# A hybrid decoder layer on one core: last shifted tokens gathered in a tile and stored as rows, and one page of indexer keys per unit

## The chip, the cores and the metric

The kernel runs on one core of a Trainium2 chip. The metric is the time of one execution on the device in microseconds (us); the median of three runs is given. Engines are named as in the profile: PE (TensorE matmul; PEld its weight load), DVE (VectorE), ACT (ScalarE), POOL (GpSimd) and SP (SyncE, which here issues nearly all DMAs).

## The reference, cut to what matters

One inference step of one layer: a prompt of 2048 tokens and, beside it, eight samples of one new token each. The layer projects its input once and splits the columns between two groups of heads, a sparse attention and an RWKV-7 recurrence; their outputs are concatenated, projected and added back.

```python
def rwkv_branch(xs, prev_row, S0, gate, mu_shift, ...):
    prev = concatenate([prev_row, xs[:, :-1]], axis=1)   # each token beside the one before
    xm = xs + mu_shift * (prev - xs)                     # the token shift
    r, k, v, wd, ad = split(xm, [512, 1024, 1536, 1600])
    ...
    S_new, y = wkv_scan(S0, r, decay, k_mod, v, -kk, kk * a_h)
    ...
    return out, S_new, xs[:, -1:]                        # xs[:, -1:] is shift_prompt

# samples: the attention's indexer reads all past keys, through a table of pages
kidx_all = concatenate([cache_kidx[page_table].reshape(8, 4096, 64), ki_s], axis=1)
```

Two things here concern the change. `xs` has 1664 columns, which the kernel holds as 13 chunks of 128 (four each for r, k and v, one for wd and ad), and its last token, `xs[:, -1:]`, is an output of 1664 numbers, `shift_prompt`. And the samples' indexer keys are gathered page by page, 32 gathers of 256 KB, before the samples' scores can be computed.

## The kernel before, in words

The prompt's tokens are cut in eight stretches `u` of 256 tokens. The RWKV heads go in four pairs `p` of heads, so that the first long phase of the program, up to about 1455 us, runs over 32 units (p, u). Each unit goes through five steps. `g_front` projects the three shifted chunks of the pair and its gate (fp16 matmuls with a high and a low part, L196 and L204), writes the result into the tile `raw` with the chunk's columns on partitions and 257 tokens along the free axis, and mixes each token with the one before it (`xm`, L512). `g_elem` computes decay and normalisations. `g_chunk` multiplies within chunks of 16 tokens and sends the small matrices through DRAM: eight stores into `asc` (L643), eight loads into `As` (L647), then on POOL a chain of one copy (L650) and 15 pairs of a multiply (L655) and an add (L656) that solves a triangular system in `Us`, then eight stores into `tsc` (L658) and one load into `TT` (L661). `g_inv` transposes `TT` (L672 on DVE) and finishes the inverse with matmuls on PE (L680 to L708). `g_tail` updates the state (L772), makes the output (L782 to L814) and stores it (`mixd`, L815). Between these steps stand pieces of other projections as fillers; weights are prefetched through `wst` (load L178, conversions on ACT L181 and DVE L182). `out_ki_p`, `Kd`, `qTd`, `gd`, `vd` and `wdad` are intermediate results or outputs that other jobs store. After the units come the sparse attention of the prompt, with the samples' work as its background, and the output projection; this second phase runs from about 1460 us to the end, and no line of it is changed.

The order on each engine is not written out by hand. A scheduler sets it from the code's order, from priorities (`later(n)` moves a piece by n) and from a timeline that it works out; `after(x, [y])` adds that x must stand behind y in the order. At run time every engine works through its own list strictly in order, and SP's list is one queue: a DMA whose condition isn't met holds every DMA behind it.

**The last tokens.** At the last stretch of each pair (u = 7) `g_front` stores the last token of each of the three chunks straight from `raw` (L518): a column of 128 partitions with one number of 4 bytes each, into 512 contiguous bytes of `out_shift_p`. One more such column, of the chunk that all pairs share, is stored by `g_ad` (L469). That makes 13 DMAs. `raw` has one buffer: the next pair's `g_pair` begins by setting its first token to zero on DVE (memset L489), and that must wait until the stores of the pair before have read it.

**The pages.** `s_pages` is a generator that gathers one page of the samples' indexer keys per step: an indirect DMA issued by POOL into the tile `pg` (L1461), then an SP store of the tile into `kxd` in DRAM (L1462). `pg` has one buffer, so that each gather waits for the store before it. `g_phase` takes two steps (`PG = 2`) in each unit, but the scheduler has issued all 32 by 468 us. `kxd` is first read (L1472) at 1482 us.

The samples' own shifted row, `out_shift_s<-sx` (L1702), is another output with another layout, and isn't changed. `So` (L789) is the small tile through which a pair's final state leaves, with one buffer in the pool `be`.

Of the kernel before, what the change touches and what calls it, by code (L numbers as in the profile page):

```python
# [9 lines left out]
F32 = mybir.dt.float32  # L10
# [6 lines left out]
OP = mybir.AluOpType  # L17
# [14 lines left out]
GT = 256  # L32
# [8 lines left out]
class Kern:  # L41
# [166 lines left out]
    def phase_g(self):  # L208
# [7 lines left out]
        with ExitStack() as es:  # L216
# [107 lines left out]
                prefetch()  # L324
            for _ in pages:
                pass
            self.A.activation(self.sg, self.sgr, AF.Tanh, scale=0.5)
            V.tensor_scalar(self.sg, self.sg, 0.5, 0.5, op0=OP.mult, op1=OP.add)
            V.tensor_tensor(self.sg, self.sg, self.sgr, op=OP.mult)
# [30 lines left out]
    def consts_g(self, bs):  # L360
# [33 lines left out]
                    self.A.activation(self.lor[i, 2 + n], t[i], AF.Copy, scale=WS)  # L394

        self.wdad = self.dr.tile([128, 3, T], F16, name="wdad")
        self.raw12 = bs.tile([128, GT + 1], F32, name="raw12")
        V.memset(self.raw12[:, 0:1], 0.0)
        self.lwx = bs.tile([128, NCH, 65], F32, name="lwx")
# [49 lines left out]
    def g_ad(self, u, w):  # L449

        V, A, SY = self.V, self.A, self.SY
        sl = slice(u * GT, (u + 1) * GT)
        raw, out = self.raw12, self.be.tile([128, GT], F32, name="wo", tag="ta", bufs=1)
        (pg, _, _), = self.gemm_u(u, w, [self.sx[:, 12]])
        if u:
            V.tensor_copy(raw[:, 0:1], raw[:, GT:])
        A.activation(raw[:, 1:], pg, AF.Copy, scale=1.0 / WS)
        A.activation(out, pg, AF.Copy, scale=self.omu[:, 12:13])
        V.scalar_tensor_tensor(out, raw[:, 0:GT], self.pb[:, 12:13], out, op0=OP.mult, op1=OP.add)
        A.activation(out[0:64], out[0:64], AF.Tanh)  # L460
        hl = self.be.tile([128, 2, GT], F16, name="whl", tag="ksq", bufs=1)
        A.copy(hl[:, 0], out)
        self.G.tensor_tensor(hl[:, 1], out, hl[:, 0], op=OP.subtract)
        for j in range(2):
            for d in range(2):
                SY.dma_start(self.wdad[64 * d:64 * d + 64, j, sl], hl[64 * j:64 * j + 64, 0])
        SY.dma_start(self.wdad[:, 2, sl], hl[:, 1])
        if u == T // GT - 1:
            SY.dma_start(self.a["o_shift_p"][12 * 128:13 * 128].rearrange("(p o) -> p o", o=1), raw[:, GT:])  # L469

    def g_ga(self, j, i, w):

# [19 lines left out]
    def g_front(self, st, u, w0, w1):  # L492
# [20 lines left out]
                if 2 * b + c0 + n == 4:  # L513
                    self.silu(gate, pg[:, (n - 1) * GT:])
        if u == T // GT - 1:
            for j in range(3):
                c0 = (4 * j + p) * 128
                SY.dma_start(self.a["o_shift_p"][c0:c0 + 128].rearrange("(p o) -> p o", o=1), raw[:, j, GT:])  # L518
        return dict(st=st, u=u, xm=xm, gate=gate, i=p * (T // GT) + u)

    def rsqrt(self, x):
# [86 lines left out]
    def g_chunk(self, cx):  # L608
# [35 lines left out]
                         UA[16 * n:16 * n + 16, n // 4, :, :, 0, q:q + 16].rearrange("p a h t -> p (a h) t"))  # L644
        As = bv.tile([128, 16, 16], F32, name="As", bufs=2)
        for n in range(8):
            SY.dma_start(As[16 * n:16 * n + 16], bass.AP(tensor=asc.tensor, offset=asc.offset + 1024 * n,  # L647
                                                         ap=[[0, 4], [256, 4], [1, 256]]))
        Us = bv.tile([128, 4, 16], F32, name="Us", bufs=2)
        G.tensor_copy(Us, self.uinit)  # L650
# [1 line left out]
        for j in range(15):  # L652
            m, w = j // 4 + 1, 15 - j
            sh = [128, m, w]
            G.tensor_tensor(Ut[:, 0:m, j + 1:], bc(As[:, j:j + 1, j + 1:], sh), bc(Us[:, 0:m, j:j + 1], sh), op=OP.mult)  # L655
            G.tensor_tensor(Us[:, 0:m, j + 1:], Us[:, 0:m, j + 1:], Ut[:, 0:m, j + 1:], op=OP.add)  # L656
        for n in range(8):
            SY.dma_start(bass.AP(tensor=tsc.tensor, offset=tsc.offset + 16 * n * 256 + 16 * (n % 4),  # L658
                                 ap=[[256, 4], [64, 4], [1024, 4], [1, 16]]), Us[16 * n:16 * n + 16])
# [786 lines left out]
    def s_pages(self, p):  # L1446
# [11 lines left out]
        yield  # L1458
        for n in range(32):
            t = p.tile([128, 512], F32, name="pg", bufs=1)  # L1460
            G.indirect_dma_start(out=t, out_offset=None, in_=rows, in_offset=bass.IndirectOffsetOnAxis(ap=it[:, n:n + 1], axis=0))  # L1461
            SY.dma_start(self.kxd[n // 4, 8 * (n % 4):8 * (n % 4) + 8].rearrange("j (q d) k -> (j q) (d k)", q=16), t)  # L1462
            yield

    def s_scores(self, p):
        nc, V, A, G, PE, SY = self.nc, self.V, self.A, self.G, self.PE, self.SY
# [366 lines left out]
PB = 6  # L1833
P_LD = -3000
P_SC = 0
FILL = lambda k: 4 + (52 * (k + 1) + 28) // 29
F0, F1 = 1, 4
YB = 2
PG = 2
XTB, SQB = 3, 3  # L1840
X0 = 2
SQP = (0, 2)
# [217 lines left out]
```

## Time and profile before

| | |
|---|---|
| time, median of 3 runs | 2457.18 us (2455.85 to 2461.61) |
| profiled execution | 2460.94 us |
| its span in the trace | 2459.1 us, mean granted PE clock 0.925 |
| PE busy | 2108.7 us, 86% |
| DVE, ACT, POOL busy | 1611.1, 1060.8, 1097.0 us |
| the units' phase, about | 0 to 1455 us |
| stores `out_shift_p<-raw` | 13, of 0.5 KB each |
| page gathers and page stores | 32 and 32, of 256 KB each |

The page of the profile lists busy times, which are sums over the whole span; the waits, the chain of work that ended last and the table by windows tell at which place an engine stood and what released it. In a row of the windows stand the window, its length, then for PE, PEld, DVE, ACT and POOL the busy time with the number of instructions, then the TensorE clock granted (1.00 is full speed), the busy share of the 16 DMA engines, and GB/s. In a row of the timeline stand the start, the time, the engine, the line and operation, and in brackets how long the engine had idled and what ended it.

### The profile page before, as it was taken

To read this page: it belongs to the slowest core of one execution; us is meant where nothing else is said; L and a number is where in the kernel's file an instruction comes from. 1 tells how busy PE (TensorE), PEld (TensorE's weight loads), DVE (VectorE), ACT (ScalarE), POOL (GpSimd) and SP (SyncE) were. 2 spreads that over 40 slices of the span, in tenths; PEclk is the share of its full clock that TensorE was granted. 3 is DMA by queue.
4 is the path that set the end of the run, shared out by engine and by line. 5 is a ranking of instruction groups with operands and counts; after the bars stand their busy time and mean duration, and the time that the engine had idled before them with its cause. 6 is when DMAs were issued, how large, how long until landed. Compare 5 with 4: busy or idle time off the path is not lost.

```text
span 2459.1 us, 55537 instructions
## 1 busy us (share of the span) xinstructions
PE 2108.7 (86%) x20799; PEld 1497.6 (61%) x20799; DVE 1611.1 (66%) x4998; ACT 1060.8 (43%) x2243; POOL 1097.0 (45%) x2841
## 2 busy tenths in 40 slices
PE   6788998699998999979998756998887789888997
PEld 1656777587776788868876432455555445455553
DVE  4883576586775766767876776867787744556531
ACT  1652223232332333322322345888767543665530
POOL 2311345334343243232343326357767765577722
PEclk9898999899999999989999676999889999998999
DMA  6435332311112211132111412312000033220133
GB/s 223 153 113 133 96 106 92 85 51 34 33 48 42 54 51 36 49 62 58 42 37 27 130 29 70 101 58 64 10 27 10 18 84 97 65 59 27 49 104 100
DMA packets 232537, 167.59 MB, mean 68 GB/s; under 512 B 108327, under 2 KB 193280, under 8 KB 232129
## 3 DMA queue, kind: packets, MB, share of 16 engines
q1 hardware_dynamic: 226817, 149.27, 21.8%
q0 software_dynamic: 3328, 10.49, 1.6%
q8 instruction: 165, 2.70, 0.5%
q10 hardware_dynamic: 2112, 4.19, 0.5%
q14 instruction: 115, 0.94, 0.1%
HBM read 113.87 MB, written 50.00 MB: 67 GB/s over the span
## 4 chain that ended last, share of the span: by engine, by line
PE 33%; POOL 22%; DVE 11%; DMA 11%; issue 9%; SPq 7%; ACT 5%; POOLq 0%; DVEq 0%; ACTq 0%
PE ps_g L196 8%; PE ps_s L1341 5%; SPq L647 3%; POOL Us L656 3%; POOL Ut L655 3%; PE ps_l L1031 3%; PE ps_v L1281 2%; PE ps_g L204 2%; PE ps_t L1273 2%; SPq L658 2%; PE ps_g L159 2%; ACT bias L1092 2%; DMA As<-asc 1%; DVE sc L1049 1%; PE ps_e L622 1%
## 5 line engine op out<-in xcount | busy, mean ns | idle before, releaser
L196 PE MATMUL ps_g<-h,w 128*128 128x256 f16 (+1 forms) x4032 | 512.0, 281 | 34.0 <-ACT sgr L356 8.1
L196 PEld LDWEIGHTS <-w 128*128 128x128 f16 x4032 | 394.7, 101 | 105.0 <-issue 31.2
L204 PE MATMUL ps_g<-w,h 128*128 128x256 f16 (+1 forms) x2304 | 251.8, 263 | 3.0 <-ACT nat L848 2.4
L655 POOL TENSOR_TENSOR Ut<-As,Us 128x12 f32<-128x12 f32 (+10 forms) x480 | 130.8, 273 | 260.1 <-DMA As<-asc 217.7
L1252 DVE CUSTOM_DVE_ANT_0 P<-ps_l,bias 128x1024 f32<-128x1024 f32 (+7 forms) x192 | 172.5, 908 | 106.2 <-PE ps_l L1031 61.4
L204 PEld LDWEIGHTS <-h 128*128 128x128 f16 (+1 forms) x2448 | 210.1, 99 | 35.9 <-issue 8.1
L1273 PE MATMUL ps_t<-cf,P 128*128 128x128 f32 x1088 | 185.3, 298 | 32.4 <-ACT P L1260 21.4
L1276 ACT COPY pT<-ps_t 128x512 f32<-128x512 f32 (+1 forms) x288 | 154.0, 560 | 128.7 <-PE ps_t L1273 125.3
L1049 DVE SCALAR_TENSOR_TENSOR sc<-r,wi,sc 128x1024 f32<-128x1024 f32 (+7 forms) x154 | 167.7, 1089 | 37.2 <-ACT r L1048 36.4
L1260 ACT ACTIVATE P<-P,mx 128x1024 f32<-128x1024 f32 (+7 forms) x192 | 171.5, 896 | 39.9 <-DVE mx L1258 39.6
L1273 PEld LDWEIGHTS ps_t<-cf,P 128*128 128x128 f32 x1088 | 130.0, 149 | 89.7 <-ACT P L1260 28.3
L1281 PE MATMUL ps_v<-pT,Vn 128*64 128x128 f32 x2176 | 162.7, 292 | 21.8 <-ACT pT L1276 21.2
L1341 PE MATMUL ps_s<-wo,mt 128*128 128x512 f16 x768 | 172.4, 379 | 7.8 <-DVE t L1345 6.3
L1048 ACT ACTIVATE r<-ps_l 128x1024 f32<-128x1024 f32 (+7 forms) x176 | 142.4, 816 | 76.4 <-PE ps_l L1031 48.5
L1031 PE MATMUL ps_l<-K,qiT 128*128 128x512 f16 (+3 forms) x608 | 154.9, 379 | 23.7 <-ACT r L1048 12.3
L1031 PE MATMUL ps_l<-K,qT 128*128 128x512 f16 (+3 forms) x640 | 155.4, 365 | 19.2 <-ACT r L1048 12.9
L1281 PEld LDWEIGHTS ps_v<-pT,Vn 128*64 128x64 f32 x2176 | 123.2, 143 | 70.3 <-ACT pT L1276 36.8
L1092 ACT ACTIVATE bias<-sc,sm 128x640 uint8<-128x640 f32 (+13 forms) x84 | 109.9, 1308 | 129.5 <-POOL sm L1123 113.3
L656 POOL TENSOR_TENSOR Us<-Us,Ut 128x12 f32<-128x12 f32 (+10 forms) x480 | 133.9, 279 | 34.7
L1341 PEld LDWEIGHTS <-mt 128*128 128x128 f16 x768 | 74.7, 98 | 96.0 <-issue 9.0
L1031 PEld LDWEIGHTS <-qT 128*128 128x128 f16 x640 | 64.7, 104 | 79.5 <-issue 40.8
L1031 PEld LDWEIGHTS <-qiT 128*128 128x128 f16 x608 | 61.6, 106 | 83.2 <-issue 48.9
(561 smaller groups left out, 4234.2 us busy)
## 6 DMA issues: line engine op xcount, KB each, us to landing
wst<-in_wt SPq DMA_DIRECT2D x60, 256.0 KB
xt<-in_xT SPq DMA_DIRECT2D x16, 512.0 KB
wa<-in_w_ada SPq DMA_DIRECT2D x8, 1024.0 KB
kxd<-pg SPq DMA_DIRECT2D x32, 256.0 KB
qTd<-qo SPq DMA_DIRECT2D x32, 256.0 KB
kx<-kxd SPq DMA_DIRECT2D x64, 128.0 KB
mt<-mixd SPq DMA_DIRECT2D x16, 512.0 KB
x<-in_x SPq DMA_DIRECT2D x32, 256.0 KB
```

Of the source, the lines that this page charges most:

```text
L196: self.PE.matmul(out, w[:, a, k], h[:, b, k], start=(n == 0), stop=(n == 3 * KD - 1))
L204: self.PE.matmul(out, h[:, b, k], w[:, a, k], start=(n == 0), stop=(n == 3 * KD - 1))
L655: G.tensor_tensor(Ut[:, 0:m, j + 1:], bc(As[:, j:j + 1, j + 1:], sh), bc(Us[:, 0:m, j:j + 1], sh), op=OP.mult)
L656: G.tensor_tensor(Us[:, 0:m, j + 1:], Us[:, 0:m, j + 1:], Ut[:, 0:m, j + 1:], op=OP.add)
L1031: self.PE.matmul(ps[:, j:j + m], qs, self.K[:, kk, c0 + j:c0 + j + m], start=st, stop=not st)
L1049: self.dve = V.scalar_tensor_tensor(sc[:, c:c + n], r[:, :n], wi[:, h:h + 1], self.tz[:, c:c + n] if h == 0 else sc[:, c:c + n], op0=OP.mu ...
L1092: self.after(A.activation(ja[:, :L], sc[:, :L], AF.Sign, bias=t, accum_out=col(5)), [self.act])
L1252: self.dve = V.tensor_tensor_reduce(P[n][:, :w], pl[:, :w], bias[:, c:c + w], scale=1.0, scalar=-3.0e38, op0=OP.add, op1=OP.max, accum_out ...
L1260: self.act = A.activation(P[n][:, :w], P[n][:, :w], AF.Exp, scale=0.125, bias=mx[:, h, 2:3], accum_out=sums[:, n, h:h + 1])
L1273: PE.transpose(pt[:, q:q + 128], Ps[g][k // 8][:, k % 8 * 128:(k % 8 + 1) * 128], self.ident)
L1281: mm = PE.matmul(pv[64 * g:64 * g + 64, hh * 128:(hh + 1) * 128], self.Vn[:, k, 64 * g:64 * g + 64], pT[:, q + g * 128:q + g * 128 + 128], ...
L1341: PE.matmul(pg, mt[:, b, k], self.wo[:, a, k, js], start=(n == 0), stop=(n == 3 * KD - 1))
```

## The change

The 13 column stores go. A tile `shp` of 128 partitions and 13 columns takes the last tokens instead: DVE copies one column in `g_ad` and three columns at once in `g_front`, at the same places at which the stores were issued. When the loop over the units has been written, one PE transpose turns `shp` into 13 rows of 128, DVE copies these out of PSUM into `sho`, and one SP store writes 13 rows of 512 bytes. `sho` uses the buffer of `So` (tag "So", one buffer), and the three steps have a priority 40 places earlier (`P_SH`).

The pages go one per unit (`PG = 1`) instead of two. Each gather must stand behind the last add of the newest unit's `Us` chain (`h_us`), and each store is issued a unit later, behind the last `As` load (`h_as`) of that next unit's `g_chunk`.

```diff
 g_phase, behind the loop over units:
+            with self.later(P_SH):
+                pt = self.bank("m", 2)
+                PE.transpose(pt[0:13, 0:128], self.shp, self.ident)
+                t = self.be.tile([13, 128], F32, name="sho", tag="So", bufs=1)
+                V.tensor_copy(t, pt[0:13, 0:128])
+                SY.dma_start(self.a["o_shift_p"].rearrange("(c p) -> c p", p=128), t)
 setup:
+        self.shp = bs.tile([128, 13], F32, name="shp")
 g_ad:
         if u == T // GT - 1:
-            SY.dma_start(self.a["o_shift_p"][12 * 128:13 * 128].rearrange("(p o) -> p o", o=1), raw[:, GT:])
+            V.tensor_copy(self.shp[:, 12:13], raw[:, GT:])
 g_front:
         if u == T // GT - 1:
-            for j in range(3):
-                c0 = (4 * j + p) * 128
-                SY.dma_start(self.a["o_shift_p"][c0:c0 + 128].rearrange("(p o) -> p o", o=1), raw[:, j, GT:])
+            V.tensor_copy(self.shp[:, p:p + 9:4], raw[:, :, GT])
 g_chunk:
-            SY.dma_start(As[16 * n:16 * n + 16], ...)
+            self.h_as = SY.dma_start(As[16 * n:16 * n + 16], ...)
...
-            G.tensor_tensor(Us[:, 0:m, j + 1:], Us[:, 0:m, j + 1:], Ut[:, 0:m, j + 1:], op=OP.add)
+            self.h_us = G.tensor_tensor(Us[:, 0:m, j + 1:], Us[:, 0:m, j + 1:], Ut[:, 0:m, j + 1:], op=OP.add)
 s_pages:
         for n in range(32):
             t = p.tile([128, 512], F32, name="pg", bufs=1)
-            G.indirect_dma_start(out=t, ..., in_=rows, in_offset=...)
-            SY.dma_start(self.kxd[...], t)
+            ld = G.indirect_dma_start(out=t, ..., in_=rows, in_offset=...)
+            self.after(ld, [self.h_us])
             yield
+
+            st = SY.dma_start(self.kxd[...], t)
+            self.after(st, [self.h_as])
 constants:
+P_SH = -40
-PG = 2
+PG = 1
```

In the rows below the line number stands first; the lines of the changed kernel have moved down by 5 to 9, so that L643, L647, L658 and L661 of before are L648, L652, L663 and L666 there, and L1461 and L1462 are L1466 and L1470.

The first place is SP's queue at the end of the second pair (p = 1, u = 7). Before:

```order
L518 DMA out_shift_p<-raw 128x1
L815 DMA mixd<-ym 256x1x256
L643 DMA asc_77<-UA 16x4x16 x8
L647 DMA As<-asc_77 16x1x256 x8
L518 DMA out_shift_p<-raw 128x1 x2
L178 DMA wst<-in_wt 128x512 x6
L658 DMA tsc_79<-Us 16x4x16 x8
```

The same place in the changed kernel:

```order
L648 DMA asc_77<-UA 16x4x16 x8
L652 DMA As<-asc_77 16x1x256 x8
L1470 DMA kxd<-pg 128x512
L178 DMA wst<-in_wt 128x512 x2
L820 DMA mixd<-ym 256x1x256
L178 DMA wst<-in_wt 128x512 x2
L663 DMA tsc_79<-Us 16x4x16 x8
```

The three column stores are gone, and a page's store stands behind the eight `As` loads, where none stood in this unit before.

The second place is POOL's list in one of the first units. Before, a gather stands inside the `Us` chain (and two more in the rest of the same chain):

```order
L655 TENSOR_TENSOR Ut<-As,Us 128x15
L656 TENSOR_TENSOR Us<-Us,Ut 128x15
L655 TENSOR_TENSOR Ut<-As,Us 128x14
L656 TENSOR_TENSOR Us<-Us,Ut 128x14
L655 TENSOR_TENSOR Ut<-As,Us 128x13
L1461 DMA pg<-in_kidxT,pgi 128x512
L656 TENSOR_TENSOR Us<-Us,Ut 128x13
```

In the changed kernel the end of a chain, and what follows it:

```order
L661 TENSOR_TENSOR Us<-Us,Ut 128x4x2
L660 TENSOR_TENSOR Ut<-As,Us 128x4
L661 TENSOR_TENSOR Us<-Us,Ut 128x4
L1466 DMA pg<-in_kidxT,pgi 128x512
L904 TENSOR_TENSOR ru<-nat,cg 128x128
L905 TENSOR_TENSOR rv<-nat,cg 128x8x8
```

The chain is unbroken, and one gather stands behind its last add, ahead of POOL's other work of the unit (`ru` and `rv` belong to a rotary job) and of the next unit's chain.

The third place is DVE's list in the last unit (`gx` is the group normalisation of the unit's output `Y`). Before:

```order
L795 TENSOR_REDUCE gx<-ps_m 128x4
L789 COPY So<-ps_m 64x128
L796 TENSOR_SCALAR gx<-gx 128x4
L799 TENSOR_TENSOR UA<-ps_m,gx 128x256
L803 TENSOR_REDUCE gx<-Y 128x4
L804 TENSOR_SCALAR gx<-gx 128x4
```

In the changed kernel:

```order
L800 TENSOR_REDUCE gx<-ps_m 128x4
L794 COPY So<-ps_m 64x128
L801 TENSOR_SCALAR gx<-gx 128x4
L804 TENSOR_TENSOR UA<-ps_m,gx 128x256
L808 TENSOR_REDUCE gx<-Y 128x4
L331 COPY sho<-ps_m 13x128
L809 TENSOR_SCALAR gx<-gx 128x4
```

The copy into `sho` stands between the second reduction and the rest of the normalisation, four rows behind the copy into `So` whose buffer it takes over.

More of the change, by code (lines that the diff above doesn't have):

```diff
@@ L646, in g_chunk @@
         for n in range(8):
-            SY.dma_start(As[16 * n:16 * n + 16], bass.AP(tensor=asc.tensor, offset=asc.offset + 1024 * n,
+            self.h_as = SY.dma_start(As[16 * n:16 * n + 16], bass.AP(tensor=asc.tensor, offset=asc.offset + 1024 * n,
                                                          ap=[[0, 4], [256, 4], [1, 256]]))
@@ L1460, in s_pages @@
             t = p.tile([128, 512], F32, name="pg", bufs=1)
-            G.indirect_dma_start(out=t, out_offset=None, in_=rows, in_offset=bass.IndirectOffsetOnAxis(ap=it[:, n:n + 1], axis=0))
-            SY.dma_start(self.kxd[n // 4, 8 * (n % 4):8 * (n % 4) + 8].rearrange("j (q d) k -> (j q) (d k)", q=16), t)
+            ld = G.indirect_dma_start(out=t, out_offset=None, in_=rows, in_offset=bass.IndirectOffsetOnAxis(ap=it[:, n:n + 1], axis=0))
+            self.after(ld, [self.h_us])
             yield
+            st = SY.dma_start(self.kxd[n // 4, 8 * (n % 4):8 * (n % 4) + 8].rearrange("j (q d) k -> (j q) (d k)", q=16), t)
+            self.after(st, [self.h_as])
     def s_scores(self, p):
```

## The prediction

> **What bounds the kernel now.** I read the busy times by windows over the two phases first, then PE's timeline for its idle gaps, then the waits and the chain of work at each gap.
>
> ```profile
> 220.00:420.00 200.00, 190.35 (x2097) 156.65 (x2098) 125.02 (x416) 55.81 (x140) 75.43 (x198) 0.95 0.36 106
> 800.00:1075.00 275.00, 270.00 (x3361) 223.52 (x3356) 197.63 (x664) 94.83 (x235) 97.95 (x296) 1.00 0.18 47
> 1460.00:2459.00 999.00, 831.84 (x6087) 487.70 (x6087) 608.83 (x1680) 573.70 (x1074) 607.52 (x1478) 0.92 0.20 58
> ```
>
> PE is the bound: in an ordinary stretch of the units it works 190.35 of 200 us (with pages) and 270.00 of 275 us (without); in the attention's phase it works 831.84 of 999. What it loses in the units' phase it loses in a few gaps. These five windows lie one in each gap:
>
> ```profile
> 210.00:215.00 5.00, 0.00 (x0) 0.00 (x0) 0.00 (x0) 0.00 (x0) 0.00 (x0) 0.59 0.99 49
> 450.00:455.00 5.00, 0.00 (x0) 0.00 (x0) 0.43 (x1) 0.00 (x0) 1.80 (x3) 0.50 0.93 46
> 785.00:790.00 5.00, 0.00 (x0) 0.00 (x0) 0.00 (x0) 0.00 (x0) 3.71 (x17) 0.77 1.28 34
> 1080.00:1085.00 5.00, 0.00 (x0) 0.00 (x0) 0.00 (x0) 0.00 (x0) 3.67 (x18) 0.63 0.96 20
> 1345.00:1350.00 5.00, 0.00 (x0) 0.00 (x0) 0.00 (x0) 0.00 (x0) 0.00 (x0) 0.75 0.46 51
> ```
>
> PE, ACT and DVE stand nearly still, while the DMA engines count as busy (0.93 to 1.28 in four of five) and move 20 to 51 GB/s, which is what they move at a share of 0.18 in the ordinary stretch (47 GB/s). Something small is holding all sixteen. PE's rows that end these gaps:
>
> ```profile
> 216.75 0.61 PE L196 MATMUL ps_g<-h,w 128*128 128x256 f16 x2 [8.14 <-ACT sgr L356]
> ...
> 458.85 0.64 PE L708 MATMUL ps_t<-TT,g 32*32 32x32 f32 x16 [13.47 <-ACT g L704]
> 463.43 2.07 PE L622 MATMUL ps_e<-AV,BK 64*128 64x128 f32 x8 [3.94 <-DVE UA L627]
> ...
> 794.55 0.64 PE L708 MATMUL ps_t<-TT,g 32*32 32x32 f32 x16 [11.56 <-ACT g L704]
> ...
> 1089.27 0.43 PE L680 MATMUL ps_t<-tr,UA 16*32 16x32 f32 x14 [10.86 <-DVE ko L889]
> ...
> 1354.44 0.53 PE L680 MATMUL ps_t<-tr,UA 16*32 16x32 f32 x18 [11.53 <-DVE tr L672]
> ```
>
> Together 8.14 + 17.41 + 11.56 + 10.86 + 11.53 = 59.5 us. What stands behind each gap, from the waits, SP's and ACT's timelines and the chain:
>
> ```profile
> 206.00 0.46 SPq L469 DMA_DIRECT2D out_shift_p<-raw  x1
> 206.54 0.39 SPq L178 DMA_DIRECT2D wst<-in_wt  x1
> 216.07 0.63 ACT L181 ACTIVATE w<-wst 128x512 f16<-128x512 f32 x1 [10.10 <-DMA wst<-in_wt]
> ...
> 433.55 10.00 issue
> ...
> DVE gx L795 <- DMA out_shift_p<-raw: 14.4, 1, 14.4
> ...
> DVE gx L530 <- DMA out_shift_p<-raw: 12.0, 1, 12.0
> 1078.45 8.66 DMA out_shift_p<-raw
> ...
> 1343.66 10.04 DMA out_shift_s<-sx
> ...
> 1344.36 0.33 SPq L661 DMA_DIRECT2D TT<-tsc  x1
> DVE tr L672 <- DMA TT<-tsc: 72.4, 25, 12.4
> ...
> 1059.96 1.45 DMA tsc<-Us
> 1061.61 2.06 DMA TT<-tsc
> 205.10 2.09 DMA kxd<-pg
> ```
>
> Every gap follows a column store. Away from these stores a `TT` load lands in 2.06 us and a 256 KB page store in 2.09 us; two column stores of 512 bytes each take 8.66 us. The harm takes three forms. At 785 and 1080 us DVE waits outright (14.4 and 12.0 us; these rows name `gx`, but beside them stands the memset L489 of `raw`'s next pair, which must not run before the stores have read it). At 210 and 1345 us nobody needs the store, but a DMA issued just behind it is late: `wst` of 206.54 keeps ACT until 216.07, `TT` of 1344.36 keeps DVE 12.4 us. At 450 us both meet the pages: SP is held 10.00 us by a page store whose gather is late, the `tsc` stores stand behind it, and then two more column stores surround the `TT` load.
>
> The Trainium skill has a rule that speaks against this reading: its page "DMA: Bandwidth & Descriptors", section "Anatomy of one DMA — SWDGE (gpsimd) path", gives a DMA some 2 us plus bytes by 436 GB/s, for another issuing path, so 512 bytes would cost about 2 us and block nothing. The trace disagrees with 8.66 us for the pair. By the rule it would be the second rival below.
>
> **The change part by part.** First, 13 stores less. The idle time that returns is each gap less what is late next. At 210 us: `wst` behind no column store should land like other 256 KB transfers, between 2.09 us (page store) and 3.4 us (page gather, row below); 206.0 + 3.4 = 209.4, ACT could begin 6.7 us sooner, and I take 6.1. At 450 us: the hold of 10.00 us and the late `TT` go; left are the `tsc` and `TT` landings of 1.45 + 2.06, some 3 of the 17.41 us with the rest of PE's work, so 14.4. At 785 us no DMA is needed for DVE to go on; 1 us left, 10.6. At 1080 us likewise, where nearly all of the 10.86 is one wait, 10.5. At 1345 us the same `tsc` and `TT` landings and 0.6 us for the transpose are left, 4.1 us, so 7.4. Sum 49.0.
>
> Second, the clock. After each gap PE works at a lower granted clock:
>
> ```profile
> 216.00:225.00 9.00, 7.09 (x33) 4.37 (x33) 3.24 (x6) 3.26 (x7) 0.97 (x1) 0.53 0.71 208
> 458.00:470.00 12.00, 7.21 (x56) 6.06 (x56) 8.10 (x22) 4.22 (x10) 2.40 (x2) 0.50 0.48 136
> 794.00:800.00 6.00, 5.45 (x48) 3.98 (x50) 4.46 (x17) 3.14 (x8) 0.00 (x0) 0.67 0.42 119
> 1088.00:1100.00 12.00, 9.05 (x106) 6.62 (x107) 9.02 (x36) 4.23 (x12) 1.51 (x5) 0.57 0.42 109
> 1354.00:1380.00 26.00, 22.45 (x237) 18.32 (x238) 20.64 (x81) 5.63 (x17) 1.39 (x5) 0.50 0.83 268
> ```
>
> PE's busy time times the missing clock is 3.3, 3.6, 1.8, 3.9 and 11.2 us. More than DVE leaves free in the window (its length less DVE's busy time: 5.8, 3.9, 1.5, 3.0, 5.4) can't return, so at most 3.3 + 3.6 + 1.5 + 3.0 + 5.4 = 16.8. Since short gaps stay, I take two thirds, 11. The Trainium skill ("TensorE: Matmul & The Clock Gate", section "What's actually happening") puts the restart at some 3.4 us at half rate, which would make 1.7 us each and 8.5 us in all; the rows at 1.00 elsewhere and 0.50 here agree in kind and show longer restarts, 26 us of it in the last.
>
> Third, the pages. Before, they load the first ten units; now one goes with each unit.
>
> ```profile
> POOL pg L1461 <- DMA kxd<-pg: 80.6, 20, 12.8
> L1461 POOL DMA_INDIRECT pg<-in_kidxT,pgi x32: 943/990/1514, 189.0 to 463.4; - x32
> DMA to landing us min/median/max: 3.2/3.4/4.3
> L1462 SPq DMA_DIRECT2D kxd<-pg x32: 319/332/446, 192.8 to 467.7; - x32
> ...
> L500 DVE COPY raw<-raw x28: 105/169/630, 124.8 to 1317.0; 128x3 f32<-128x3 f32 x28
> ...
> POOL Ut L655 <- DMA As<-asc: 217.7, 25, 23.2
> ```
>
> Gone from the first units are the 80.6 us for which POOL stood inside or between its chains and the SP holds of the page stores. PE hardly felt it: it idles 9.65 of 200 us with pages and 5.00 of 275 without, so at the second rate 200 us would have 3.6, so at most 9.65 − 3.6 = 6 us return; I take 2, since the hold at 433.55 is counted already. In the later units, some 24, each page adds 0.99 us to POOL behind its chain and 0.33 us to SP behind `As`. POOL's cover is its own wait for `As`, 217.7 us in 25 units or 8.7 us each; without that cover a later chain would start 0.99 us later, 24 us in all as the far end. The page stands a unit in its buffer, so the store finds it landed and holds nobody on SP: behind it stand `wd`, `gd`, `mixd` and `wst`, and then `tsc`, which waits for POOL's whole chain. I take 0. The traffic of a page beside the `tsc` stores and the `TT` load has no row of its own: the bounds are 0 and its landing of 3.4 us (a rival below). Near 0 is the nearer row, because the units from 220 us carried three pages each and PE still worked 190.35 of 200 us.
>
> Fourth, what is added. Five DVE copies of at most three columns cost 0.17 us each by the row of `raw`'s own three-column copy, so under 1 us. At the end stand a transpose, a copy and a store:
>
> ```profile
> 1454.41 0.65 SPq L790 DMA_DIRECT2D out_S_p<-So  x1
> 1455.53 0.42 DVE L803 TENSOR_REDUCE gx<-Y 128x4 f32<-128x256 f32 x1 [0.54 <-ACT Y L802]
> ```
>
> `sho` takes `So`'s buffer, so DVE waits there for the landing of the store issued at 1454.41. Issue 0.65 and a landing of 1.45 to 2.09 give 1456.5 to 1457.2; DVE arrives at 1455.95, waits 0.6 to 1.2 us and copies 0.3. Behind it stand the rest of `gx` and the output of the last unit, on the path: 1.5 us. The two last gathers stand back to back, the second waiting for the first one's store, about 2.1 us on POOL beside the attention's start: 0.5 us. Together 2 us.
>
> The attention phase is reordered by the scheduler though no work is added. PE idles 167 of its 999 us there, and a reorder can give some of that back or add to it; I allow a tenth, 17 us, either way for the range and take 0, since nothing in the rows says which.
>
> Sum: −49 − 11 − 2 + 2 = −60. Against the profiled execution of 2460.94 us (span 2459.1) that is 2401; the median of the runs lies 3.8 us below that execution, and I say 2400. A measurement of this kernel can tell about 0.3%, 7.4 us, from no change.
>
> **The rivals.**
>
> *Only the outright waits go.* What is late next at 210, 450 and 1345 us is no column store but the queue itself: six `wst` loads, the `K` loads, or the `tsc` and `TT` chain. For it: at 1345 us the DMA share is 0.46, half of the other gaps', and the chain names `out_shift_s` with 10.04 us, a store that stays. Against it: `out_shift_s` has 104 numbers, 416 bytes, per partition, not 4, and three column stores of the pair stand just ahead of it in SP's queue. Then only 10.6 + 10.5 return with two thirds of 4.5 us of clock (1.5 + 3.0) and 2 of pages: −26, giving 2434.
>
> *The column stores are not the cause.* If 13 stores of 512 bytes block nothing, the gaps stay wherever something else holds the DMA engines, and what goes is the page's hold of 10.00 us: 2450. Against it: two DVE waits named by the trace for these stores, and gaps at 785 and 1080 us where no page runs.
>
> *Slower: a page beside every inverse.* The gather is issued just as the eight `tsc` stores and the `TT` load of the same unit go out. DVE waits for `TT` in 25 units already, 2.9 us each. If the page's 3.4 us go onto this wait and PE stands for it, 24 further units cost 82 us: 2461 − 60 + 82 = 2483. It decides from 60 / 24 = 2.5 us a unit. Against it: PE's share with three pages a unit.
>
> *More than forecast.* All of the 59.5 us, all 16.8 of clock and 6 of pages return, with 2 us of cost: −80, giving 2381.
>
> **How the numbers follow.** The forecast of about 2400, within 17 us for the attention's reorder: 0.68. Only the outright waits: 0.14. More: 0.06. Column stores not the cause: 0.07, half of it within 0.3%. Page beside every inverse: 0.05, of which a fifth stays near no change. Faster 0.68 + 0.14 + 0.06 + 0.035 = 0.915, same 0.045, slower 0.04. The range reaches down to the full return, 2380 in round numbers, and up over the outright waits alone, 2436; above it lie 0.12, below some 0.04.
>
> **What would show it.** In the trace of the changed kernel no `out_shift_p<-raw` row; the windows at the five pair ends filled, with no PE gap over 5 us there; granted clock 0.9 or more behind them; the memset of `raw` with no wait; first phase ending near 1395 us instead of 1455. The wait for `TT` at or below 72.4 us. It would be wrong if gaps of 8 us or more remain with `wst`, `K` or `TT` as releaser, if the wait for `TT` grows by 60 us, or if the attention phase lengthens by over 17 us.

## The result, and the profile after

The changed kernel takes 2375.62 us (median of 4 runs, 2372.52 to 2376.78), against 2456.51 us before (4 runs): a ratio of 0.9665, 95% interval 0.9648 to 0.9681. It is faster, by 81 us where the prediction said 57, and lies 4 us under the range. The profiled execution took 2375.91 us with a span of 2374.1; the two spans differ by 85.0 us.

The same windows as before, over the places where the columns had been stored, and the one long gap of PE that is left, from the windows and PE's timeline of the changed kernel:

```profile
205.00:215.00 10.00, 7.81 (x67) 6.08 (x65) 3.04 (x6) 3.33 (x7) 0.00 (x0) 1.00 0.57 170
415.00:435.00 20.00, 16.18 (x203) 12.63 (x201) 17.64 (x54) 9.75 (x24) 5.12 (x6) 0.83 0.35 101
725.00:740.00 15.00, 15.00 (x220) 12.96 (x219) 8.58 (x28) 6.99 (x20) 5.31 (x21) 1.00 0.29 85
1005.00:1020.00 15.00, 11.83 (x145) 10.29 (x146) 9.30 (x37) 2.52 (x8) 3.56 (x12) 1.00 0.33 96
1315.00:1325.00 10.00, 0.00 (x0) 0.00 (x0) 0.00 (x0) 0.00 (x0) 7.37 (x33) 0.69 0.33 94
```

```profile
1326.15 0.65 PE L685 MATMUL ps_t<-tr,UA 16*32 16x32 f32 x32 [11.89 <-DVE tr L677]
```

Four of the five places hold work again: PE is busy for 78 to 100% of them, at a granted clock of 0.83 to 1.00, where it had stood still. The fifth is as empty as before. To see where the time went I cut each execution at the four copies of a pair's final state (`So`), which stand at the end of each pair in every order, and sum the windows between them. Before, then after:

```profile
170.00:602.28 432.28, 384.77 (x4313) 318.61 (x4311) 276.07 (x933) 134.92 (x329) 155.91 (x408) 0.94 0.31 84
602.28:892.17 289.89, 265.16 (x3348) 217.28 (x3347) 201.46 (x696) 95.32 (x232) 100.62 (x296) 0.96 0.20 47
892.17:1202.35 310.18, 292.64 (x3672) 244.88 (x3673) 222.35 (x817) 96.03 (x255) 104.34 (x343) 0.97 0.20 49
1202.35:1454.11 251.76, 211.46 (x2755) 158.28 (x2753) 182.72 (x597) 83.92 (x196) 81.95 (x257) 0.87 0.20 54
```

```profile
170.00:565.37 395.37, 378.20 (x4329) 313.83 (x4328) 276.30 (x939) 134.68 (x328) 132.02 (x376) 0.97 0.22 61
565.37:836.13 270.76, 262.66 (x3369) 216.74 (x3367) 205.33 (x700) 97.39 (x237) 112.72 (x312) 0.99 0.23 64
836.13:1134.05 297.92, 287.94 (x3624) 241.46 (x3624) 216.34 (x810) 92.53 (x246) 115.20 (x352) 0.99 0.24 66
1134.05:1384.31 250.26, 212.13 (x2756) 159.78 (x2753) 182.91 (x600) 84.75 (x200) 91.71 (x264) 0.87 0.25 71
```

The second number of a row is the pair's length, the third PE's busy time. The pairs became shorter by 36.9, 19.1, 12.3 and 1.5 us, 69.8 in all. PE's idle time in them (length less busy time) fell from 47.5, 24.7, 17.5 and 40.3 us to 17.2, 8.1, 10.0 and 38.1; the clock rose in the first three and not in the last. The remaining 15 us came off the attention's phase, from PE's first matmul after its first long wait (1479.91 before, 1410.51 after) to the end: 979.2 us before, 963.6 after.

### The profile page after: what moved, and what is told of

Read it like the earlier page. It is cut to its first block, busy times and chain, and to the rows that moved or that the text cites. A ratio compares the mean times of both kernels' runs of the same rounds, so it can differ in the third digit from the quotient of the medians.

```text
span 2374.1 us, 55529 instructions
## 1 busy us (share of the span) xinstructions
PE 2094.2 (88%) x20800; PEld 1486.4 (63%) x20800; DVE 1614.7 (68%) x5004; ACT 1059.1 (45%) x2243; POOL 1110.7 (47%) x2841
## 4 chain that ended last, share of the span: by engine, by line
PE 41%; POOL 20%; DVE 11%; issue 8%; DMA 8%; SPq 7%; ACT 5%; POOLq 0%; DVEq 0%; ACTq 0%
PE ps_g L196 9%; PE ps_s L1346 6%; PE ps_l L1036 4%; PE ps_g L204 3%; POOL Ut L660 3%; POOL Us L661 3%; PE ps_v L1286 3%; SPq L652 3%; PE ps_t L1278 2%; PE ps_g L159 2%; PE ps_e L627 2%; DMA As<-asc 2%; SPq L663 2%; SPq L648 1%; ACT bias L1097 1%
## 5 line engine op out<-in xcount | busy, mean ns | idle before, releaser
L196 PE MATMUL ps_g<-h,w 128*128 128x256 f16 (+1 forms) x4032 | 502.2, 277 | 26.4 <-ACT h L453 7.0
L660 POOL TENSOR_TENSOR Ut<-As,Us 128x12 f32<-128x12 f32 (+10 forms) x480 | 135.2, 282 | 302.1 <-DMA As<-asc 269.7
L1286 PE MATMUL ps_v<-pT,Vn 128*64 128x128 f32 x2176 | 161.8, 290 | 25.6 <-ACT pT L1281 25.2
L1036 PE MATMUL ps_l<-K,qiT 128*128 128x512 f16 (+3 forms) x608 | 157.7, 386 | 22.6 <-DVE mx L1257 12.8
L1036 PE MATMUL ps_l<-K,qT 128*128 128x512 f16 (+3 forms) x640 | 155.4, 367 | 13.9 <-ACT r L1053 9.5
L661 POOL TENSOR_TENSOR Us<-Us,Ut 128x12 f32<-128x12 f32 (+10 forms) x480 | 130.9, 273 | 34.7
```

Of the source, the lines that this page charges most:

```text
L196: self.PE.matmul(out, w[:, a, k], h[:, b, k], start=(n == 0), stop=(n == 3 * KD - 1))
L661: self.h_us = G.tensor_tensor(Us[:, 0:m, j + 1:], Us[:, 0:m, j + 1:], Ut[:, 0:m, j + 1:], op=OP.add)
L1036: self.PE.matmul(ps[:, j:j + m], qs, self.K[:, kk, c0 + j:c0 + j + m], start=st, stop=not st)
L1286: mm = PE.matmul(pv[64 * g:64 * g + 64, hh * 128:(hh + 1) * 128], self.Vn[:, k, 64 * g:64 * g + 64], pT[:, q + g * 128:q + g * 128 + 128], ...
```

## The experiments

All are told by the same two lengths of their profiled execution: the end of the units' phase (the last `So` copy) and the attention's phase as just defined. In these comparisons the kernel before took 2449 to 2453 us instead of 2456.5, so times are compared as ratios to it. Where I say that PE's order is the same, the list of its instructions is the same row for row. Each length is that of one execution. Two executions of before's order, `before` and `before_bg1300` (told below), end the units' phase at 1454.1 and 1443.3 us, and two of the changed kernel's order, the changed kernel and `after_bg1300`, at 1384.3 and 1389.0. So a difference of less than some 10 us between two single executions shows little.

### The two halves of the change

`shift_only` is the changed kernel with the pages put back:

```diff
-            ld = G.indirect_dma_start(...); self.after(ld, [self.h_us])
-            yield
-            st = SY.dma_start(self.kxd[...], t); self.after(st, [self.h_as])
+            G.indirect_dma_start(...); SY.dma_start(self.kxd[...], t)
+            yield
-PG = 1
+PG = 2
```

> The gathered last tokens alone; the pages as before, two per unit. Theory (the column stores hold the DMA engines, and the pages in the first units cost some 12 us beside that): the gaps at the ends of pairs 1 and 2 go (-19 and -12 us, as in the changed kernel), the first pair gives back some 25 of the 37 us, the last pair 2, and the attention's phase, which the scheduler orders anew in every variant, lies within 15 us either way: 2398, between 2383 and 2413. Rival (the pages make the gaps of the first pair, the column stores only DVE's two waits): -33, 2424.

`pages_only` is the kernel before with the pages of the change and the 13 column stores.

> One page per unit alone; the 13 column stores as before. Theory: DVE's waits of 12 to 14 us at the memset of raw stay, the windows at the pair ends stay empty, only the first pair's pages give back some 12 us: 2445, between 2430 and 2460 with the attention's reorder. Rival: -37 at the first pair, nothing more, 2420.

Measured: `shift_only` 2382.46 us, ratio 0.9724 (0.9698 to 0.975); `pages_only` 2418.15 us, 0.9869 (0.9843 to 0.9895). The units' phase ends at 1405.5 and 1434.7, the attention takes 954.0 and 962.3 us. So the gathered last tokens give 48.6 us of the units' phase and the pages 19.4, which together is nearly the 69.8 of both (each would be 10.8 less against the other execution of before's order); and the attention is shorter in both than before's 979.2, by 25.2 and 16.9 us. In the units' phase the theory had expected 58 and 12, and nothing of the attention. In the total, `shift_only` lies just under its expected range and `pages_only` 12 us under it, beside the rival's 2420. The rival does not gain by that: it had put 37 us on the first pair, which gave 16.0, and 16.9 of the total came from the attention's phase. In `pages_only` DVE still stands at the column stores, 12.8 us at the end of the second pair (p = 1) and 9.5 at the end of the third.

### What a column store does

`spread` has the order of `pages_only` on PE and differs in where a column goes:

```diff
-SY.dma_start(self.a["o_shift_p"][c0:c0 + 128].rearrange("(p o) -> p o", o=1), raw[:, j, GT:])
+SY.dma_start(self.shd[4 * j + p, :, 0:1], raw[:, j, GT:])     # shd: [13, 128, 128] f32 in DRAM
```

> As pages_only in the order of every instruction, but each column of 128 numbers is stored into a scratch tensor with 512 bytes between two numbers instead of 512 bytes in a row (the output of the last tokens is left unwritten). If the harm is that 128 writes of 4 bytes meet in the same 512 bytes of DRAM, the store lands in some 2 us, the gaps go and the time is some 65 us below pages_only, near 2380. If each write of 4 bytes is slow by itself, the time is that of pages_only within 5 us and the DVE waits stay at 12 to 14 us.

Measured: 2371.69 us, ratio 0.9682 (0.9656 to 0.9707), 46.5 us below `pages_only` where some 65 had been expected. Same stores, same number of 4-byte pieces, same place in every queue, and the units' phase ends at 1390.6 instead of 1434.7. The two stores that stand together at the end of the second pair, from SP's and DVE's timelines and the windows, in `pages_only`:

```profile
759.46 0.85 SPq L518 DMA_DIRECT2D out_shift_p<-raw  x2
...
768.64 0.42 DVE L795 TENSOR_REDUCE gx<-ps_m 128x4 f32<-128x256 f32 x1 [12.79 <-DMA out_shift_p<-raw]
768.64 0.06 DVE L489 MEMSET raw<- 128x3 f32 x1
```

```profile
760.00:765.00 5.00, 0.00 (x0) 0.00 (x0) 0.00 (x0) 0.00 (x0) 2.85 (x13) 0.89 0.99 75
```

and in `spread`:

```profile
734.64 0.85 SPq L519 DMA_DIRECT2D shd<-raw  x2
...
736.71 0.06 DVE L490 MEMSET raw<- 128x3 f32 x1
```

```profile
735.00:740.00 5.00, 5.00 (x90) 4.28 (x88) 2.94 (x11) 1.65 (x5) 2.73 (x13) 1.00 0.54 166
```

The memset that waits for the stores starts 8.3 us after their issue ended (768.64 less 760.31) in the one and 1.2 us (736.71 less 735.49) in the other, without a wait on DVE. In the one the DMA engines are busy at 0.99 and move 75 GB/s while PE stands; in the other they are busy at 0.54 and move 166. The harm is the meeting of 128 small writes in one place of DRAM, not their number. It doesn't add up store by store either: at the end of the third pair of `pages_only` three of them stand together, and DVE goes on 8.5 us after the last issue. One more thing differs, since `spread` writes into a scratch tensor instead of the output; the next run writes into a scratch tensor too and is slow again, so the tensor alone is not the reason.

`lines64` keeps 16 numbers of a column together and sets the groups 512 bytes apart:

```diff
+bass.AP(tensor=shd.tensor, offset=shd.offset + 1024 * (4 * j + p), ap=[[128, 8], [1, 16], [1, 1]])
```

> As spread, but the 128 numbers of a column are stored as 8 groups of 16: the 16 numbers of a group fill 64 bytes in a row, and the groups lie 512 bytes apart (the output of the last tokens is left unwritten). If the writes of 4 bytes disturb each other within 64 bytes, the stores land as late as in pages_only (8 us a pair), DVE waits 10 us or more at the memset of raw, and the time is near 2418. If they disturb each other within 512 bytes, an eighth meets in one place: landing within 3 us, DVE waits under 2 us, near 2375.

Measured: 2403.08 us, 0.9798 (0.9768 to 0.9828), in an order of its own up to the attention and in before's order from there on; the units' phase ends at 1397.9, the attention takes 979.9. The memset at the end of the second pair starts 4.9 us after the issue ended (SP 731.71 + 1.33, DVE 737.97):

```profile
731.71 1.33 SPq L519 DMA_DIRECT2D shd<-raw  x2
...
737.97 0.42 DVE L796 TENSOR_REDUCE gx<-ps_m 128x4 f32<-128x256 f32 x1 [4.49 <-DMA shd<-raw]
```

That is between both expectations. Either neighbours within 64 bytes disturb each other, though less than all 128 in a row, or the other shape of the transfer has a part in it (a pair's issue took 1.33 us instead of 0.85). At which distance the harm ends is not settled.

`before_spread` spreads the columns of the kernel before as `spread` does (512 bytes between two numbers) and keeps its order on PE entirely:

> The kernel before in its own order (PE's list is the same row for row), with each column of 128 numbers stored into a scratch tensor, 512 bytes between two numbers (the output of the last tokens is left unwritten). It prices the column stores by themselves. Theory: the gaps at 210, 785 and 1080 us and the column's part of the one at 450 us go, the one near 1345 us shrinks or moves; the units' phase ends 44 to 50 us sooner than 1454, near 1407, and the attention's phase, which follows its order alone, stays at 977 to 980: 2410. Rival (the attention's 15 us hang on the units' phase ending undisturbed): the attention's phase falls to 965 or less, 2395.

Measured: 2403.36 us, 0.9807 (0.9778 to 0.9835); units' phase to 1400.1, attention 975.7.

```profile
170.00:579.60 409.60, 378.64 (x4292) 314.45 (x4290) 274.09 (x931) 133.19 (x327) 155.64 (x408) 0.97 0.31 89
579.60:854.38 274.78, 263.49 (x3348) 216.62 (x3347) 201.59 (x697) 95.11 (x232) 101.75 (x296) 0.98 0.18 50
854.38:1157.76 303.38, 294.73 (x3671) 246.88 (x3672) 222.04 (x816) 95.68 (x255) 106.12 (x344) 0.98 0.18 50
1157.76:1400.14 242.38, 208.14 (x2756) 156.28 (x2754) 182.49 (x598) 83.54 (x196) 79.64 (x256) 0.89 0.20 56
```

The theory held in the main: the units' phase is shorter by 54.0 us where 44 to 50 were expected, and the attention keeps its length, which refutes the rival. This prices the column stores alone: 22.7, 15.1, 6.8 and 9.4 us in the four pairs. Against the other execution of before's order (`before_bg1300`) it is 20.2, 9.5, 6.2 and 7.2, or 43.1 together, and the medians of the whole kernel differ by 47.0. What the change gained beyond that in the units' phase, 15.8 us, belongs to the pages and to the order that came with them; from `before_spread` to `spread`, which differ in the pages alone, it is 9.5. Of these, 14.2 and 13.9 us lie in the first pair (409.6 less 395.4 and 395.7). That part is no chance of one execution: the first pair takes 408 to 421 us in the three kernels that send all pages through POOL in the first units and store no column in one stretch (`before_spread`, `shift_only`, `nohold`), and 394 to 397 in the eight others that store none. In the other three pairs the differences have both signs.

### What a page costs

`free_gather` drops one line of the change, `store_now` two:

```diff
 free_gather:
-            self.after(ld, [self.h_us])
 store_now:
-            yield
             st = SY.dma_start(self.kxd[...], t)
-            self.after(st, [self.h_as])
+            yield
```

> The changed kernel without the order of the gathers behind the Us chain: one page per unit, each stored a unit later, but the gather now stands inside the chain, behind its third multiply, as before the change. Theory (the 20 us that the pages cost are SP standing still at page stores whose gather is under way, 87.5 us in all): nothing of that comes back, and the units' phase ends within 4 us of the changed kernel's 1384. Rival (a gather inside the chain makes the chain and so TT late): 1 us per unit on PE's path, the phase ends near 1410.

> The changed kernel with each page's store written right behind its gather instead of a unit later: on SP it stands between the eight tsc stores and the TT load. Theory (SP's hold at page stores is the price): the gather lands some 4.5 us after the chain and the tsc stores take 3.9 us to issue, so SP is held by under 1 us a unit, and the units' phase ends 0 to 10 us later than 1384. Rival (the deferral of the store is what matters little, the number per unit everything): no difference, within 3 us.

Measured: `free_gather` 2392.8 us, 0.9773 (0.9731 to 0.9815), units' phase to 1403.3; `store_now` 2404.8 us, 0.9809 (0.977 to 0.9849), units' phase to 1399.4. My theory missed in both: the units' phase is 18.9 and 15.1 us longer than the changed kernel's. In `free_gather` the gather stands inside the chain, whose unit has just sent the store that must free its buffer, and in three units the chain waits for it, for 8.7 to 15.1 us. Yet the first pair, with one of these waits, loses nothing (394.2 us against 395.4), and the second, with one of 10.0, loses 20 (291.0 against 270.8); so the rival's price of 1 us in each unit isn't borne out either. From the waits of the changed kernel, of `free_gather` and of `store_now`:

```profile
POOL Ut L660 <- DMA As<-asc: 269.7, 27, 28.0
DVE tr L677 <- DMA TT<-tsc: 47.9, 21, 12.1
```

```profile
POOL Ut L660 <- DMA kxd<-pg: 33.8, 3, 15.1
DVE tr L677 <- DMA TT<-tsc: 60.6, 24, 12.9
```

```profile
SPq L1468 <- DMA pg<-in_kidxT,pgi: 5.6, 2, 4.9
POOL Ut L660 <- DMA As<-asc: 308.6, 25, 29.5
```

In `free_gather` DVE waits 60.6 us for `TT` where the changed kernel has 47.9. In `store_now` SP is held for only 5.6 us, as the theory had it, and yet it is 15 us later, with 308.6 us of POOL waiting for `As` against 269.7. PE's order is another one in both, and I can't say which of its moves costs what: the second pair takes 284.0 us in `shift_only` too, which has no page there. So what each of the two orders is worth by itself isn't shown.

That left three suspects for the 14 us of the first pair: SP standing at page stores, the traffic, and the gathers in POOL's chain. `nohold` stores a constant tile instead of the gathered page, so that SP waits for nothing and the bytes stay; `nopool` drops the gathers and copies the keys with SP from DRAM to DRAM:

```diff
 nohold (from before_spread):
+            ld = G.indirect_dma_start(...); self.after(ld, [previous store])
+            st = SY.dma_start(self.kxd[...], bc(self.cf[:, None, 0:256], [128, 2, 256])); self.after(st, [ld])
 nopool (from nohold, PG = 5):
-            ld = G.indirect_dma_start(...)
+            ld = SY.dma_start(self.kxs[n]..., rows[128 * n:128 * n + 128]...); self.after(ld, [self.h_as])
```

> As before_spread (columns stored with 512 bytes between two numbers, pages at their old places in the first units), but each page's store sends a constant tile instead of the gathered page (the samples' keys are left out, and so is the output of the last tokens): the same bytes go both ways at about the same places, and SP and POOL wait for nothing. If the pages' price in the first pair is SP held by stores that wait for gathers (89.0 us in 23 waits), the first pair's state is copied at 568 us or sooner instead of 579.6, as in the changed kernel (565.4). If it is the traffic, or the gathers in POOL's chain, it stays at 576 or later.

> As nohold (constant tiles stored as pages, columns stored with 512 bytes between two numbers), but without any gather on POOL: SP copies 256 KB of keys from DRAM to a scratch tensor instead, five such pairs of transfers in each of the first seven units, behind the As loads (the samples' keys and the output of the last tokens are left out). The traffic is about that of before, POOL's chains are unbroken, SP is held by no gather. If the pages' price in the first units is POOL's chain, broken by gathers that wait for one buffer (61.9 us of waits in nohold), the first pair's state is copied at 570 us or sooner, against 590.7 in nohold and 579.6 in before_spread. If it is the traffic, it stays at 578 or later.

Measured: `nohold` 2403.51 us, 0.9817 (0.979 to 0.9844), first pair to 590.7; `nopool` 2385.44 us, 0.9749 (0.972 to 0.9777), first pair to 566.6. The window from 170 to 480 us in `before_spread`, then in `nopool`:

```profile
170.00:480.00 310.00, 281.97 (x3141) 233.21 (x3139) 196.42 (x649) 97.35 (x242) 112.34 (x288) 0.96 0.35 104
```

```profile
170.00:480.00 310.00, 293.00 (x3294) 243.86 (x3293) 206.24 (x690) 103.68 (x255) 87.25 (x262) 0.98 0.34 102
```

The traffic is the same (104 and 102 GB/s), and PE works 11 us more. So the traffic is cleared. SP's hold is cleared too: `nohold` has none and loses another 11 us, in an order on PE of its own. What is left is the gathers on POOL, several in a unit, that wait for one buffer inside and between the chains on which the inverses depend, and without them the first pair is as short as in the changed kernel. One such wait stands in the kernel before, in the middle of a chain, from POOL's timeline:

```profile
432.94 0.27 POOL L655 TENSOR_TENSOR Ut<-As,Us 128x12 f32<-128x12 f32 x1
439.91 1.23 POOL L1461 DMA_INDIRECT pg<-in_kidxT,pgi  x1 [6.71 <-DMA kxd<-pg]
441.15 0.23 POOL L656 TENSOR_TENSOR Us<-Us,Ut 128x12 f32<-128x12 f32 x1
```

The page store that it waits for went out at 431.50 us, just ahead of a column store at 431.93, so both costs meet here. The hold of SP that the prediction read at 433.55 us is for the page store of this very gather; it begins on POOL. From `nohold`'s waits, the first row over the whole program, the second over 170 to 480 us:

```profile
POOL pg L1462 <- DMA pg<-in_kidxT,pgi: 61.9, 26, 4.2
SPq L659 <- POOL Us L657: 51.6, 7, 12.4
```

POOL stands 61.9 us in 26 waits for the one buffer, and SP's `tsc` stores stand 51.6 us for POOL's chains, against 23.2 us in the same window of `nopool`. On PE it shows as waits for the transposed `TT` of a unit's inverse, from the waits over 170 to 565 us of `before_spread`, `nohold` and the changed kernel:

```profile
PE ps_t L681 <- DVE tr L673: 6.3, 3, 3.8
PE ps_t L681 <- DVE tr L673: 8.6, 2, 5.3
PE ps_t L685 <- DVE tr L677: 0.8, 1, 0.8
```

In `nopool` it is 0.6. The rest of what PE idles more in the first pair is spread over shorter waits.

### What is left at the last pair

`late_loads` orders the attention's first loads behind the `As` loads of the last but one unit:

```diff
+        self.after(<each load of K, Vn, ca, tz, qiT, qT>, [self.h_ass[30]])
```

> The changed kernel, with the attention's first loads (K, Vn, ca, tz, qiT, qT) ordered behind the As loads of the last but one unit. Theory (the gap of 11.9 us left at 1326 is an As load that stands in SP's queue behind those loads and lands 5.9 us after its issue): As lands some 8 us sooner, the gap falls to 4 us or less, the units' phase ends 6 to 10 us sooner, in all 2367, with up to 15 us either way from the attention's reorder. Rival (the gap is POOL's chain of 14 us beside DVE's work): the gap stays above 9 us.

Measured: 2385.49 us, 0.9729 (0.9698 to 0.9759); units' phase to 1387.3, attention 973.2. The gap does shrink, and another grows behind it:

```profile
1319.88 0.65 PE L687 MATMUL ps_t<-tr,UA 16*32 16x32 f32 x32 [5.28 <-DVE tr L679]
1351.58 0.65 PE L687 MATMUL ps_t<-tr,UA 16*32 16x32 f32 x32 [8.60 <-DVE tr L679]
```

The last pair gains 3.0 us, and the whole is not faster. Both expectations missed: the first gap fell below the rival's 9 us and not to the theory's 4, and the units' phase did not end sooner. What sets the length of the last pair stays open.

### The attention's phase

`after_bg1300` and `before_bg1300` are the changed kernel and the one before with `P_BG = 1300`.

> The changed kernel with another priority for the background work of the attention phase (P_BG 1300 instead of 1500): the order of PE's instructions up to the attention is the same row for row, from there on it is another. Theory (the 15 us that the attention's phase became shorter are the luck of an order, since five orders so far took 954 to 973 us and before's 979): the units' phase ends within 3 us of 1384, the attention's phase differs from 964 us by 3 to 15 us either way. Rival (the 15 us come from the change itself): the attention's phase stays within 3 us of 964.

> The kernel before with the same other priority (P_BG 1300): PE's order up to the attention is that of before row for row. Theory: the units' phase ends within 3 us of 1454, and the attention's phase falls from 979 us towards the 954 to 973 us of the other orders, by 6 us or more. Rival (something of the units' phase of before makes its attention slow): it stays within 3 us of 979.

Measured: 2378.35 us, 0.9696 (0.9661 to 0.9731), and 2451.54 us, 0.9999 (0.9974 to 1.0025); attention 962.7 and 976.8 us. My expectation missed in both: the attention's length hardly moved. But the test was weak, since the constant moves only one or two in a hundred of PE's 6087 matmuls in that phase. It missed in the units' phase too, which should have ended within 3 us of 1384 and 1454 and ended at 1389.0 and 1443.3, with PE's order up to there unchanged; that is how far single executions of one order lie apart. The other runs say more of the attention. PE's rows of that phase by windows, in the order before, after, `shift_only` and `store_now`, all of them with 6087 matmuls:

```profile
1480.00:2459.00 979.00, 831.75 (x6087) 487.59 (x6087) 595.76 (x1617) 565.94 (x1062) 592.76 (x1444) 0.92 0.21 59
```

```profile
1410.50:2374.00 963.50, 829.32 (x6087) 482.47 (x6087) 601.66 (x1617) 564.61 (x1062) 597.69 (x1444) 0.93 0.21 60
```

```profile
1431.70:2386.00 954.30, 825.96 (x6087) 486.36 (x6087) 594.82 (x1617) 565.82 (x1062) 595.88 (x1444) 0.93 0.21 61
```

```profile
1425.60:2404.00 978.40, 835.67 (x6087) 487.11 (x6087) 595.37 (x1617) 565.18 (x1062) 594.81 (x1444) 0.92 0.21 59
```

Some kernels share one order there row for row: before, `before_spread` and `lines64` take 979.2, 975.7 and 979.9 us, `pages_only` and `spread` 962.3 and 960.5, though their units' phases differ by up to 56 and 44 us. So the order of this phase sets its length within some 4 us, and what went before hardly touches it. Over the nine orders that differ in more than a few rows it lies between 954.0 and 979.9 (`nohold` 966.6, `nopool` 975.3), and not by the parts of the change: with the gathered tokens it is 954.0 (`shift_only`) as well as 978.4 (`store_now`). The scheduler makes a new order of this phase from most changes upstream; before had drawn one of its longest. Which moves in the order make it long stays open: PE's idle time there (147 us before, 134 after) is spread over many waits of at most 6.2 us.

## Why the prediction was right or wrong

- **The column stores, −49 of idle time and −11 of clock.** Right in mechanism and nearly in size: −54.0 in before's own order (−43.1 against its other execution). By pair, the working gave 25, 12, 12 and 11 us, and 22.7, 15.1, 6.8 and 9.4 were measured. The rule of the Trainium skill of some 2 us for a small DMA ("DMA: Bandwidth & Descriptors", section "Anatomy of one DMA — SWDGE (gpsimd) path"), given for DMAs that GpSimd issues, is far from the contiguous columns' 8.3 us a pair and near the spread ones' 1.2 us. The same page of the Trainium skill says in its section "Rules for kernel authors" that a non-contiguous last dimension makes one descriptor per element; both columns have 128 elements, and the one costs 44 us more over the program, so the number of descriptors is not the price here.
- **The gap at 1345 us, "7.4 returns".** Wrong in place. `before_spread` keeps a gap of 11.6 us there, behind an inverse that waits, and gains its 9.4 us elsewhere in the pair: a further gap of before, 7.86 us at 1402 us, which the working did not list, is gone. In the changed kernel this pair gains only 1.5, and in `shift_only`, without a page in it, 2.9, so that the pages are not shown to take the rest. Here the first rival had it right.
- **The pages, "PE hardly felt it; I take 2".** This step failed. It measured 15.8 us (19.4 and 21.2 beside the columns in one stretch and beside the gathered ones, 9.5 beside the spread ones), of which 12.5 to 16.0 lie in the first pair. The working had POOL's 80.6 us of waits in hand and bounded them by PE's idle time in one window of before, 220 to 420 us. That window reads too little: PE idles 9.65 us of it before, 15.5 in `before_spread` and 7.0 in the changed kernel. Over the whole first pair PE is busy for the same time in `before_spread` and in the changed kernel (378.6 and 378.2 us, at a clock of 0.97 in both), and its idle time is 31.0 us in the one and 17.2 in the other: all of the gain is waits. The working, and the experiments at first, sought the pages' cost in SP's holds; the runs clear them. By elimination, and by the waits of PE shown above, the cause in the first pair is the gathers that wait on POOL and make the chains and the inverses late.
- **The cost in the later units, 0.** Right in the sum: the second and third pair of the changed kernel are shorter than those of `before_spread`, by 4.0 and 5.5 us, although they carry the pages now, and the last is 7.9 us longer. DVE's wait for `TT` is 47.9 us, against 72.4 before and 60.4 in `before_spread`. The rival of a page beside every inverse, with 82 us, is refuted.
- **The end, "1.5 us" for `sho`.** The mechanism as forecast, the size smaller:

```profile
1386.70 0.28 DVE L331 COPY sho<-ps_m 13x128 f32<-13x128 f32 x1 [0.54 <-DMA out_S_p<-So]
```

  0.54 us of wait and 0.28 of copy; from `So` to the attention's first matmul it is 26.2 us instead of 25.8.
- **The attention's phase, "I take 0, 17 either way".** This term failed too: it gave 15.6 us. That is the luck of an order, since the scheduler's orders spread over 26 us and before had one of the longest. The bound held, but it stood in the forecast's own spread and not beneath the full return of the other terms; with it, the range would have reached down to some 2364 instead of 2380.

The sum as it came out in the profiled executions: −54.0 for the columns, −15.8 for the pages, +0.4 at the end and −15.6 for the attention make −85.0, the difference of the spans, against −60 in the working. No single term made the miss: the pages gave 14 us more and the attention 16, the columns 6 less. The split between columns and pages is uncertain by some 10 us, as the second executions show.

## What to carry to other kernels

When the DMA engines are busy at 0.9 and more and move a fraction of what they move elsewhere (20 to 49 GB/s here, against 268 at 0.83 between 1354 and 1380 us of the kernel before), look for a small store just before, and for 4-byte pieces that meet in one place; transposing the column once and storing it as rows cost under a microsecond here. A wait inside a dependent chain on an engine that is half idle is not free: ask what stands behind the chain, not how busy the engine is, and bound it over the whole stretch and not in one window. And where a scheduler lays out the program, a change in the first phase redraws the second: price that by its own spread (26 us here over nine orders), and compare variants that keep the order when one term is to be measured.

## What the runs showed of the hardware

- Two stores of 128 writes of 4 bytes each, every one into 512 bytes in a row, freed their source 8.3 us after their issue, three in a row 8.5 us, with the DMA engines busy at 0.99 and 75 GB/s moved, and a load issued just behind a single one (206.54 us of the kernel before) came only at 216.07. With 512 bytes between the writes DVE overwrote the source 1.2 us after the issue of two, and PE worked on. With groups of 16 in 64 bytes it was 4.9 us.
- The page traffic in the first units, with 102 GB/s moved in all from 170 to 480 us, cost PE nothing that could be seen once the gathers were off POOL: the first pair takes 396.6 us with it (`nopool`) and 395.4 in the changed kernel, where the first pair moves 61 GB/s.
